# Opening loads issued in one fixed order, by quarters, and the samples' compression moved behind the token-stationary products

## The chip, the cores and the metric

The kernel runs on one core of one Trainium2 chip. The metric is the device time of one execution in microseconds (us). Engines are named as in the profile: PE is TensorE (PEld its weight loads), DVE is VectorE, ACT is ScalarE, POOL is GpSimd, SP is SyncE, which here does little else than issue DMAs. Every engine works through its own list of instructions in order; a list is fixed when the program is built.

## The reference, cut to what matters

One layer of a decoder trunk, for a prompt of 1024 tokens and 8 samples of 4 tokens (1056 tokens, width 1024), all in float32. Of it the change concerns the opening and what reads its results:

```
sh1, sc1, g1, sh2, sc2, g2 = split(silu(c) @ W_ada + b_ada)     # per sequence: the prompt and 8 samples
u = x * (1 + sc1) + sh1
proj = u @ W_in                                                  # q, k, v, gates ... of two head groups
def compress_kv(kv, pe, w1, w2):                                 # blocks of 32 rows, stride 16
    hid = gelu(einsum(blocks(kv) + pe, w1))                      # 2048 -> 256, for k and for v
    return einsum(hid, w2)                                       # 256 -> 64
```

For the samples `compress_kv` runs over the cached rows: `cache_cmp_kv` holds pages of 128 rows, and `page_table` names two pages for each sample, 16 in all. The compressed keys and values are then attended together with selected blocks from another paged cache, a window, and the sample's own rows. Behind that come an mLSTM head group, an output projection, a layer norm and a feed-forward block.

## The kernel before

The opening (lines 213 to 303) is one stretch of code without a planner; a list scheduler orders each engine's instructions from it, by data and by buffers.

The activations `u` are kept transposed, 128 channels on the partitions, in two float32r parts whose sum is u: `uh` (rounded) and `ul` (the rest), each 128 x 8 x 1056. `split` (lines 48 to 51) makes such a pair: ACT casts, DVE subtracts. The same is done to every weight tile (`wt..h`, `wt..l`), and a product is taken as three: uh times high, ul times high, uh times low.

Channels come in four quarters, q = 0 to 3, each of the channel tiles q and q + 4. For a quarter, `ada_steps` (from line 140) loads four tiles `wada` of 512 KB and multiplies them with silu(c) on PE; the result is copied by ACT (`adasb`), transposed by PE (`adat`) and given its bias by DVE (`adaT`, then `sc1p` = 1 + scale). Then three chunks of x (384, 384 and 288 tokens, buffers `xk`) are loaded, scaled and shifted by ACT and DVE, and split into uh and ul. The narrow weight `w_a` (1024 x 288: one K and V branch and all gates) is loaded in four pieces of neighbouring channel tiles in the first quarter, and split into `ah` and `al`, 288 KB a piece.

Two things are computed from this. The token-stationary products `pA` (line 298): nine token tiles, each u (128 tokens as weights) times w_a, 24 matmuls of 288 columns, ordered so that a quarter can be used as soon as it is there; results leave through `vst` to DRAM (`d_v`) and into `gn`. And the samples' compression: `hidS` (line 277), per s (0 for keys, 1 for values) 16 products of w1 with the cached rows for two halves of the hidden layer. Its rows stand in `kv` (128 x 2 x 2 x 8 x 130), filled from the 16 cache pages (`kvr`, two pages in a buffer, four buffers) by copies on DVE and ACT. w1 is loaded in four halves of 1 MB into three buffers. For s = 0 the rows are taken in two pieces of columns (64 and 65), for s = 1 at once (129, times two heads: 258 columns). A float32 matmul shows as two passes in the profile. `gelu2` follows, and `cmp_k`, `cmp_v` (`pkS`, `pvS`) multiply by w2.

Every DMA of the opening is issued by SP, but for eight of the 16 cache pages, which ACT issues. A page's address is first read from the page table into a register. One sequence of DMAs shares eight completion counters in turn, so a DMA waits on SP until the one eight before it has landed. Behind a DMA that waits, all later ones of that engine's list wait too.

Behind the opening come the projections: `proj` takes tile by tile of W_in (order 14 to 19, 12, 13, then 20, 4, 0, 8, ...), 24 matmuls for each of three token chunks, as `pj14_0`, `pj14_1`, `pj14_2` and so on (line 354); `next_weights` loads a tile (512 KB into the single buffer `wst`) one tile ahead, and two pairs of split buffers hold it. Between the projections stand the gates' chain, the next part of ada (`ada10` to `ada13`, line 149, loaded behind the bias row's store `d_rb` and its broadcast `d_rt`), and the samples' attention: scores `SS0`, `SS1` (lines 831 to 844) for two groups of samples, each from four tiles `kb` and a value tile `SV` that take 48 loads in all (lines 839 to 842), then transposes (`ptS`, `ptT`), values (`oS`, `oT`) and an output (`mN`). Projection tiles 12 and 13 give the prompt's compressed rows, `hid` (line 492), for which `d_ck` is stored and read back as `cmpT`.

## Time and profile before

| | us |
|---|---|
| median of 3 runs | 1577.49 |
| lowest and highest run | 1574.25 and 1582.03 |
| the profiled execution | 1580.96 |
| its span in the trace | 1579.2 |

| stretch of the span | what runs on PE |
|---|---|
| 0 to 11.8 us | nothing |
| 11.8 to 51 us | hidS, with ada of the quarters in between |
| 42 to 92 us | pA, quarter by quarter |
| 92 to 183 us | projection tiles 14 to 19, second part of ada in between |
| 183 to 300 us | tiles 12, 13, 20, ..., samples' attention, prompt's compression, third part of ada |

A row of the timeline gives start, length, engine, line, operation, output and inputs, how many instructions are merged in it, and in brackets the idle time of the engine ahead of it with what ended it. A row of the windows gives a stretch, its length, busy time and count of PE, PEld, DVE, ACT and POOL, then the granted TensorE clock (1.00 is full), the busy share of the 16 DMA engines and GB/s. A row of the waits gives who waited for whom, the total, how often, and the longest.

### The profile page before, as it was taken

How to read it: one execution, taken by the hardware profiler on the slowest of the kernel's cores; microseconds unless marked ns; L12 is line 12 of the kernel's file. 1: busy time of each engine (PE TensorE's matmuls, PEld its weight loads, DVE VectorE, ACT ScalarE, POOL GpSimd, SP SyncE). 2: the span in 40 equal slices, each digit the busy share in tenths (PEclk: the TensorE clock that was granted, in tenths of full speed). 3: DMA queues.
4: the chain of work that ended last, by engine and by line, in shares of the span. 5: the costliest groups of instructions: out<-in, count | busy, mean ns of one | idle time of the engine just before them, and what ended most of it. 6: DMA issues, size and time to landing. Idle time of an engine off the chain costs nothing.

```text
span 1579.2 us, 30041 instructions
## 1 busy us (share of the span) xinstructions
PE 1494.8 (95%) x11647; PEld 1436.4 (91%) x11647; DVE 1072.5 (68%) x2366; ACT 629.0 (40%) x1258; POOL 308.6 (20%) x383
## 2 busy tenths in 40 slices
PE   6899999999999999899998799999999999998976
PEld 6789988899999998798897799999999999998975
DVE  2521131386776678977688887676768878889888
ACT  2422132375655566645367322222226433332301
POOL 0000000143224243443103300000001121103244
PEclk9989999999999999999999899999999999999988
DMA  9767566421020323323564566233315241412222
GB/s 300 267 210 241 138 203 218 138 74 47 26 81 17 110 58 113 89 68 105 169 214 155 171 225 208 97 107 109 109 69 191 99 148 57 148 55 82 82 86 84
DMA packets 112985, 204.11 MB, mean 129 GB/s; under 512 B 18529, under 2 KB 63498, under 8 KB 111914
## 3 DMA queue, kind: packets, MB, share of 16 engines
q1 hardware_dynamic: 111546, 200.87, 39.3%
q8 instruction: 92, 1.51, 0.4%
q10 hardware_dynamic: 1296, 1.31, 0.2%
q14 instruction: 51, 0.42, 0.1%
HBM read 162.95 MB, written 46.07 MB: 132 GB/s over the span
## 4 chain that ended last, share of the span: by engine, by line
PE 76%; DVE 13%; DMA 5%; issue 3%; ACT 2%; SPq 1%; POOL 0%; DVEq 0%; ACTq 0%
PE p L1308 19%; PE pj L354 16%; PE pd L1543 11%; PE po L354 6%; PE o L1060 4%; PE pt L1019 4%; PE S L979 4%; DMA wada<-in_w_ada 2%; DVE oplT L51 2%; DVE ophT L51 2%; PE pA L298 2%; PE hidS L277 2%; DVE A L1554 2%; DVE acc L1548 1%; PE ada L149 1%
## 5 line engine op out<-in xcount | busy, mean ns | idle before, releaser
L1543 PE MATMUL pd<-oplT,ophT 128*128 128x264 f32 x2352 | 292.3, 287 | 8.5 <-DVE acc L1548 4.4
L1543 PEld LDWEIGHTS pd<-oplT,ophT 128*128 128x128 f32 x2352 | 291.3, 190 | 9.4 <-DVE ophT L51 4.7
L1002 POOL TENSOR_SCALAR P<-P,l,sg 128x64 f32<-128x64 f32 (+8 forms) x192 | 129.0, 686 | 175.1 <-DVE l L999 156.3
L51 DVE TENSOR_TENSOR PTl<-pt,PTh 128x512 fp32r<-128x512 f32 (+1 forms) x160 | 102.0, 643 | 31.6 <-ACT PTh L50 31.1
L996 ACT ACTIVATE P<-P,mn 128x640 f32<-128x640 f32 (+7 forms) x128 | 94.4, 738 | 68.8 <-DVE mn L823 65.7
L354 PE MATMUL pj<-uh,wt_l 128*128 128x384 f32 (+1 forms) x576 | 120.3, 333 | 0.0
L50 ACT CAST PTh<-pt 128x512 fp32r<-128x512 f32 (+1 forms) x160 | 86.8, 550 | 79.9 <-PE pt L1019 79.0
L1554 POOL TENSOR_TENSOR A<-A,A 128x1024 f32<-128x1024 f32 x7 | 24.1, 3454 | 478.1 <-DVE ophT L51 478.1
L354 PE MATMUL pj<-uh,wt_h 128*128 128x384 f32 (+1 forms) x576 | 115.8, 331 | 1.1 <-ACT rw L468 1.1
L354 PE MATMUL pj<-ul,wt_h 128*128 128x384 f32 (+1 forms) x576 | 116.5, 329 | 0.0
L50 ACT CAST ophT<-A 128x1024 fp32r<-128x1024 f32 x49 | 51.3, 1051 | 139.7 <-PE pd L1543 92.0
L354 PEld LDWEIGHTS pj<-uh,wt_l 128*128 128x128 f32 x576 | 95.7, 190 | 2.9 <-issue 2.4
L354 PEld LDWEIGHTS pj<-uh,wt_h 128*128 128x128 f32 x576 | 93.5, 189 | 3.6 <-issue 1.6
L1019 PE MATMUL pt<-ident,P 128*128 128x128 f32 x592 | 95.5, 275 | 1.1 <-POOL P L1002 1.0
L354 PEld LDWEIGHTS pj<-ul,wt_h 128*128 128x128 f32 x576 | 94.5, 188 | 2.1 <-issue 1.6
L1548 DVE TENSOR_TENSOR acc<-acc,pd 128x264 f32<-128x264 f32 (+1 forms) x126 | 61.7, 513 | 27.6 <-PE pd L1543 27.6
L1060 PE MATMUL o<-PTh,V 128*128 128x256 f32 x264 | 78.9, 306 | 0.5 <-DVE ob L1079 0.4
L1060 PE MATMUL o<-PTl,V 128*128 128x256 f32 x264 | 72.7, 296 | 3.0 <-DVE PTl L51 2.6
L1019 PEld LDWEIGHTS pt<-ident,P 128*128 128x128 f32 x592 | 70.0, 141 | 4.5 <-POOL P L1002 1.8
L51 DVE TENSOR_TENSOR oplT<-B,oplT 128x1056 fp32r<-128x1056 f32 x49 | 72.5, 1479 | 0.4 <-ACT oplT L50 0.2
L979 PE MATMUL S<-K,QH 128*128 128x512 f32 (+3 forms) x200 | 71.6, 362 | 0.9 <-DVE mn L823 0.7
L51 DVE TENSOR_TENSOR ophT<-A,ophT 128x1024 fp32r<-128x1024 f32 x49 | 66.0, 1349 | 8.7 <-ACT ophT L50 8.7
(1095 smaller groups left out, 3465.6 us busy)
## 6 DMA issues: line engine op xcount, KB each, us to landing
wada<-in_w_ada SPq DMA_DIRECT2D x48, 512.0 KB
aw<-in_w_up SPq DMA_DIRECT2D x32, 512.0 KB
d_r<-C SPq DMA_DIRECT2D x62, 264.0 KB
B<-d_r SPq DMA_DIRECT2D x28, 528.0 KB
A<-in_w_down SPq DMA_DIRECT2D x28, 512.0 KB
wst<-in_w_t SPq DMA_DIRECT2D x24, 512.0 KB
wst<-in_w_out SPq DMA_DIRECT2D x24, 512.0 KB
w<-in_cmp_w SPq DMA_DIRECT2D x4, 1024.0 KB
```

Source lines behind the costliest of these rows:

```text
L50: nc.scalar.copy(hi, src)
L51: nc.vector.tensor_tensor(out=lo, in0=src, in1=hi.bitcast(F32), op=ALU.subtract)
L354: PE.matmul(ps[:, 0:n], lhsT=a[:, k, :], rhs=b[:, k, t0:t0 + n], start=(i == 0 and k == 0), stop=(i == 2 and k == 7))
L979: PE.matmul(S[:, 0:w], lhsT=Q[:, r], rhs=K[j][:, k0 + c0:k0 + c0 + w], start=(i == 0), stop=(i == 1))
L996: ACT.activation(P[:, o:o + n], P[:, o:o + n], AF.Exp, bias=mn[:, br:br + 1], scale=-1.0, accum_out=l[:, br:br + 1])
L1002: POOL.tensor_scalar(P[:, a:b], P[:, a:b], l[:, x:x + 1], sg[:, qb, y:y + 1], op0=ALU.mult, op1=ALU.mult)
L1019: PE.transpose(pt[:, 256 * x + 128 * e:256 * x + 128 * e + 128], P[:, o:o + 128], ident)
L1060: PE.matmul(op, lhsT=vv, rhs=ps[e][:, 256 * x:256 * x + 256], start=(x0 + x == 0 and e == 0), stop=(x0 + x == len(bl) - 1 and e == 1))
L1308: PE.matmul(ps[:, 0:HH], lhsT=w[a][:, k], rhs=ops[name][b][:, k, HH * h:HH * h + HH], start=(i == 0 and k == 0), stop=(i == 2 and k == 3))
L1543: PE.matmul(ps[h][:, 0:HH], lhsT=x[:, 128 * m:128 * m + 128], rhs=y[:, HH * h:HH * h + HH], start=(i == 0), stop=(i == len(mms) - 1))
L1548: DVE.tensor_tensor(out=out, in0=out, in1=x, op=ALU.add)
L1554: eng.tensor_tensor(out=r[out], in0=r[a], in1=r[b], op=op)
```

## The change

One chain of issue is added: `ordered` issues a DMA on SP behind the previous DMA of the chain. The opening's large loads all go through it: the four ada tiles, the three x chunks and one piece of w_a for each quarter, then the weights of projection tiles 14 and 15, then the position rows, the 16 cache pages with three of w1's halves between them, and the last half. The pages are all issued by SP. w_a is cut by quarters (channel tiles q and q + 4) in place of neighbouring tiles. The x buffers become six in place of four. The compression `hidS` stands behind the token-stationary products, and for s = 0 takes its 129 columns at once.

```diff
+    chain = []
+    def ordered(*a):
+        with tc.issue_after(chain[-1]) if chain else ExitStack():
+            chain.append(SP.dma_start(*a).ins)
...
-                SP.dma_start(w, io["w_ada"][G, c0, :, k:k + 2])
+                (SP.dma_start if G else ordered)(w, io["w_ada"][G, c0, :, k:k + 2])
...
-    WB, XB = 4, 4
+    WB, XB = 4, 6
...
-        SP.dma_start(w1[s, hf], io["cmp_w1"][:, s, 8 * hf:8 * hf + 8])
-    load_w1(0, 0)
+        ordered(w1[s, hf], io["cmp_w1"][:, s, 8 * hf:8 * hf + 8])
+    def load_caches():
+        pe_ = mk(p0, [128, 2, 2, 8, 2], F32, "pe_")
+        ordered(pe_, io["peT"])
+        DVE.tensor_copy(kvx[:, :, 128:130], pe_.rearrange("p s g c n -> p (s g c) n"))
+        for i in range(16):
+            if i % 5 == 4:
+                load_w1(*((0, 0), (0, 1), (1, 0))[i // 5])
+            page = SP.value_load(pt_sb[0:1, i:i + 1], min_val=0, max_val=19)
+            if i % 2 == 0:
+                kr = mk(p0, [128, 2, 32, 8], F32, "kvr", bufs=4, name=f"kvr{i}")
+            ordered(kr[:, i % 2], io["cache_c"][bass.ds(page, 1)].rearrange("o p (x n) -> p (o x) n", n=8))
+            if i % 2:
+                o = kvx[:, :, 8 * i - 8:8 * i + 8].rearrange("p x (a n) -> p a x n", a=2)
+                (DVE.tensor_copy if i % 4 == 1 else ACT.copy)(o, kr)
+        load_w1(1, 1)
+        SP.dma_start(w2, io["cmp_w2"])
...
-    for i in range(16):
-        e = ACT if i % 2 else SP
-        page = e.value_load(pt_sb[0:1, i:i + 1], min_val=0, max_val=19)
...
-        if i == 6:
-            load_w1(0, 1)
...
+    def next_weights(mt, load=SP.dma_start):
...
-        if q == 0:
-            load_w1(1, 0)
...
-            SP.dma_start(xk[:, :, 0:n], io["xT"][:, q::4, t0:t0 + n])
+            ordered(xk[:, :, 0:n], io["xT"][:, q::4, t0:t0 + n])
...
-        if q == 0:
-            for k in range(0, 8, 2):
-                st = mk(p0, [128, 2, 384], F32, "xk", bufs=XB, name=f"wa{k}")[:, :, 0:288]
-                SP.dma_start(st, io["w_a"][:, k:k + 2])
-                split(nc, ah[:, k:k + 2], al[:, k:k + 2], st)
-        if q == 0:
-            load_w1(1, 1)
-            SP.dma_start(w2, io["cmp_w2"])
-    for s in range(2):
...
-        for n0, n in ((0, 64), (64, 65)) if s == 0 else ((0, 129),):
...
+        st = mk(p0, [128, 2, 384], F32, "xk", bufs=XB, name=f"wa{q}")[:, :, 0:288]
+        ordered(st, io["w_a"][:, q::4])
+        split(nc, ah[:, q::4], al[:, q::4], st)
+    next_weights(14, ordered)
+    load_caches()
...
         SP.dma_start(d_v[t0:t0 + m], vst[0:m])
+    for s in range(2):
...
+        for n0, n in ((0, 129),):
```

The lists of the engines move as follows. A row gives the line, the operation, the output and inputs (the program's names with a buffer number) and the shape. In the changed program the lines stand seven further down, and an ordered DMA bears line 132.

ACT, the fourth quarter of u, before: `adasb03` is the copy of ada's result, `xk30` to `xk32` the three chunks of x, `gu0` belongs to the compression.

```order
L50 CAST uh_119<-xk22_532 128x2x288
L152 COPY adasb03_582<-ada03_540 128x128
L255 ACTIVATE xk30_587<-xk30_587,adaT_93,sc1p_103 128x384
L255 ACTIVATE xk31_593<-xk31_593,adaT_93,sc1p_103 128x384
L255 ACTIVATE xk32_599<-xk32_599,adaT_93,sc1p_103 128x256
L183 ACTIVATE gu0_677<-gu0_677 128x516
L50 CAST uh_119<-xk30_587 128x2x384
```

The same place on ACT now, where `wa3` is the fourth piece of w_a and `wst` the weights of projection tile 14:

```order
L50 CAST uh_119<-xk22_336 128x2x288
L50 CAST ah_132<-wa3_415 128x2x288
L159 COPY adasb03_390<-ada03_348 128x128
L50 CAST wt14_h_421<-wst_419 128x1024
L283 ACTIVATE xk30_395<-xk30_395,adaT_93,sc1p_103 128x384
L283 ACTIVATE xk31_401<-xk31_401,adaT_93,sc1p_103 128x384
L283 ACTIVATE xk32_407<-xk32_407,adaT_93,sc1p_103 128x256
L50 CAST uh_119<-xk30_395 128x2x384
```

The cast of the w_a piece stands ahead of ada's copy and the cast of tile 14's weights ahead of the scaling of x. DVE at the same place now:

```order
L51 TENSOR_TENSOR ul_120<-xk22_336,uh_119 128x2x288
L51 TENSOR_TENSOR al_133<-wa3_415,ah_132 128x2x288
L162 TENSOR_TENSOR adaT_93<-adat03_349,badaT_94 128x4x9
L51 TENSOR_TENSOR wt14_l_422<-wst_419,wt14_h_421 128x1024
L278 TENSOR_SCALAR sc1p_103<-adaT_93 128x2x9
L285 TENSOR_SCALAR xk30_395<-xk30_395,sc1p_103,adaT_93 128x384
```

Both splits stand among the steps that lead to the scaled x, with `sc1p` behind tile 14's; before, no weight split stood between `adaT` and `sc1p` of this quarter.

PE, the end of the token-stationary products, before (`pA8` is the last token tile, `prb` the bias row's product):

```order
L298 MATMUL pA8_961<-ah_315,ul_120 32x288 x2
L310 MATMUL prb_994<-oh_992,rb_115 8x384
L191 MATMUL pkS_1000<-hidS_317,w2_113 64x128 x2
L354 MATMUL pj14_0_1049<-uh_119,wt14_h_1039 128x384 x8
L354 MATMUL pj14_0_1049<-ul_120,wt14_h_1039 128x384 x8
L354 MATMUL pj14_0_1049<-uh_119,wt14_l_1040 128x384 x5
```

PE at the same place now:

```order
L308 MATMUL pA8_853<-ah_132,ul_120 32x288 x2
L361 MATMUL pj14_0_1017<-uh_119,wt14_h_421 128x384 x8
L361 MATMUL pj14_0_1017<-ul_120,wt14_h_421 128x384 x8
L361 MATMUL pj14_0_1017<-uh_119,wt14_l_422 128x384 x7
L319 MATMUL hidS00_882<-kv_130,w100_478 128x258 x3
L319 MATMUL hidS01_883<-kv_130,w100_478 128x258 x3
```

After these two rows come 58 more of hidS, one by one; then the rest of tile 14's first chunk and all of its second, `prb`, `pkS` and `pvS`, and only then its third. The matmuls of ada10, which stood within tile 14's third chunk, stand within tile 15's second.

SP, the samples' attention, before: `wst_2239` is the load of projection tile 13's weights, `kb` and `SV` are the attention's loads.

```order
L840 DMA SV0_1894<-in_cache_s 128x128
L789 DMA qr_1853<-d_q_81 64x4x32
L841 DMA kb02_1988<-in_cache_w 128x256
L842 DMA SV0_1894<-in_cache_w 128x256 x2
L842 DMA SV1_2064<-in_cache_w 128x256 x4
L334 DMA wst_2239<-in_w_t 128x1024
L470 DMA d_ck_83<-rw12_0_2298 128x384
L839 ISA
L839 DMA kb03_1997<-in_cache_s 128x128
```

SP now, around the load of tile 13's weights (`wst_2207`):

```order
L846 DMA kb13_2135<-in_cache_s 128x128
L847 ISA
L847 DMA SV1_2032<-in_cache_s 128x128
L848 DMA kb13_2135<-in_cache_w 128x256
L849 DMA SV1_2032<-in_cache_w 128x256
L253 DMA wst_2207<-in_w_t 128x1024
L477 DMA d_ck_83<-rw12_0_2266 128x384
L477 DMA d_ck_83<-rw12_1_2318 128x384
```

The load stood ahead of `kb03` and all of the second group's `kb`; now it stands behind all 48 loads. On PE the scores, the first group's values and `kb13` stand ahead of tile 13's first matmul in the same way.

More of the change, by code (lines that the diff above doesn't have):

```diff
@@ L215, in _body @@
     w1 = {}
[L216 removed]
+    WB, XB = 4, 6
+    kvx = kv.rearrange("p s g c n -> p (s g c) n")
     def load_w1(s, hf):
         w1[s, hf] = mk(p0, [128, 8, 256], F32, "w1", bufs=3, name=f"w1{s}{hf}")
[L220 to L227 removed]
@@ new lines, in _body, with weights @@
+    SP.dma_start(badaT, io["badaT"])
+    def weights(src, name, stage=None, tag="wst", bufs=1, load=SP.dma_start):
+        st = mk(stage or wp, [128, 1024], F32, tag, bufs=bufs, name="wst")
+        load(st, src)
+        h = mk(wp, [128, 8, 128], F32R, "wh", bufs=2, name=name + "h")
+        l = mk(wp, [128, 8, 128], F32R, "wl", bufs=2, name=name + "l")
+        split(nc, h, l, st.rearrange("p (k c) -> p k c", k=8))
+        return h, l
+    tile_order = [14, 15, 16, 17, 18, 19, 12, 13] + [x + h for h in range(4) for x in (20, 4, 0, 8)]
@@ L241, in _body @@
+    ahead = {}
+    def next_weights(mt, load=SP.dma_start):
+        i = tile_order.index(mt)
+        for x in tile_order[i:i + 2]:
+            if x not in ahead:
+                ahead[x] = weights(io["w_t"][x], f"wt{x}_", load=load)
+        return ahead[mt]
     ah = mk(pA, [128, 8, 288], F32R, "ah")
@@ L303, in _body @@
         SP.dma_start(d_v[t0:t0 + m], vst[0:m])
+    for s in range(2):
+        ph = [mk(ps0, [128, 512], F32, "ha"[s], bufs=2, name=f"hidS{s}{ht}") for ht in range(2)]
+        for n0, n in ((0, 129),):
+            for c in range(16):
+                for ht in range(2):
+                    PE.matmul(ph[ht][:, 0:258].rearrange("p (g n) -> p g n", g=2)[:, :, n0:n0 + n],
+                              lhsT=w1[s, c // 8][:, c % 8, 128 * ht:128 * ht + 128],
+                              rhs=kv[:, s, :, c % 8, n0 + c // 8:n0 + c // 8 + n],
+                              start=(c == 0), stop=(c == 15))
+        for ht in range(2):
+            ACT.copy(pehid[:, s, ht:ht + 1], ph[ht][:, 128:129])
+            ACT.activation(hidS[:, s, ht].rearrange("p g n -> p (g n)"), ph[ht][:, 0:258], AF.Identity,
+                           bias=pehid[:, s, ht:ht + 1])
+        gu = mk(p0, [128, 2, 384], F32, "xk", bufs=XB, name=f"gu{s}")
+        gelu2(gu.rearrange("p a b -> p (a b)")[:, 0:516], hidS[:, s].rearrange("p b c d -> p (b c d)"))
     DVE.memset(rb[32:33], 1.0)
@@ L330, in _body @@
     mlg = mk(ce, [128, 4], F32, "mlg")
-    def weights(src, name, stage=None, tag="wst", bufs=1):
-        st = mk(stage or wp, [128, 1024], F32, tag, bufs=bufs, name="wst")
-        SP.dma_start(st, src)
-        h = mk(wp, [128, 8, 128], F32R, "wh", bufs=2, name=name + "h")
-        l = mk(wp, [128, 8, 128], F32R, "wl", bufs=2, name=name + "l")
-        split(nc, h, l, st.rearrange("p (k c) -> p k c", k=8))
-        return h, l
-    tile_order = [14, 15, 16, 17, 18, 19, 12, 13] + [x + h for h in range(4) for x in (20, 4, 0, 8)]
-    ahead = {}
-    def next_weights(mt):
-        i = tile_order.index(mt)
-        for x in tile_order[i:i + 2]:
-            if x not in ahead:
-                ahead[x] = weights(io["w_t"][x], f"wt{x}_")
-        return ahead[mt]
     def mm24_steps(ps, w, xh, xl, t0, n):
```

23 lines of the change are left out of this document (removed).

## The prediction

> **What bounds the kernel now.** I read the page first, then the table of waits of PE for the first 300 us, then the timelines of PE, ACT, DVE and SP around each place that the change touches.
>
> ```profile
> span 1579.2 us, 30041 instructions
> PE 1494.8 (95%) x11647; PEld 1436.4 (91%) x11647; DVE 1072.5 (68%) x2366; ACT 629.0 (40%) x1258; POOL 308.6 (20%) x383
> ```
>
> PE is busy for 95% of the span. Only stretches in which PE idles can give time back, and work that is moved out of them comes back in full. The longest two entries of PE's waits in the first 300 us (reason, total, times, longest):
>
> ```profile
> PE hidS L277 <- ACT kv L236: 11.8, 1, 11.8
> PE ada L149 <- DMA wada<-in_w_ada: 8.5, 8, 2.6
> ```
>
> With the 3.8 us at 75.80 below, and without the 3.8 us of the w_ada waits that fall past 240 us, the opening holds some 20 us of idle time. The opening on PE (start, length, count, idle time ahead and its reason):
>
> ```profile
> 44.37 4.62 PE L277 MATMUL hidS<-kv,w 128*128 128x258 f32 x20 [0.41 <-DMA w<-in_cmp_w]
> 48.94 2.77 PE L277 MATMUL hidS<-kv,w 128*128 128x258 f32 x12
> 51.36 0.48 PE L298 MATMUL pA<-ah,uh 128*128 128x288 f32 x1
> 75.80 0.85 PE L298 MATMUL pA<-ah,uh 128*128 128x288 f32 x2 [3.78 <-ACT uh L50]
> 92.46 0.81 PE L310 MATMUL prb<-oh,rb 33*8 33x384 f32 x2
> 104.03 1.30 PE L354 MATMUL pj<-uh,wt_h 128*128 128x288 f32 x8
> 108.88 1.08 PE L149 MATMUL ada<-wada,sil 128*32 128x128 f32 x16 [2.61 <-DMA wada<-in_w_ada]
> ```
>
> The samples' compression (hidS) runs while the loads of w_ada and x come in. From 75.80, where the fourth quarter of u is ready, to 104.03, the first matmul of the last third of projection tile 14, PE does 28.23 us of work without a pause.
>
> **The change, term by term.** *Opening.* All of that 28.23 us is still to be done behind the fourth quarter, and now all of hidS too. The rows above put 32 passes into 44.37 to 51.36, less about 0.1 us of a transpose: 0.215 us each. Both halves of hidS are 128 passes (64 of the 192 go, since the first half is no longer cut in two): 27.5 us. So the mark at 104.03 becomes (start of the fourth quarter) + 28.2 + 27.5, and the opening gains only if that quarter starts before 48.3 us. When does it?
>
> ```profile
> 23.00:43.00 20.00, 18.20 (x181) 15.16 (x179) 6.57 (x13) 6.79 (x13) 0.00 (x0) 1.00 0.97 342
> 43.00:63.00 20.00, 19.59 (x179) 16.75 (x179) 9.17 (x18) 9.18 (x17) 0.00 (x0) 1.00 0.98 352
> 57.00:66.00 9.00, 8.67 (x99) 7.68 (x98) 5.66 (x12) 5.54 (x9) 0.00 (x0) 1.00 1.03 393
> 66.00:70.00 4.00, 4.00 (x48) 3.50 (x50) 1.34 (x5) 1.27 (x2) 0.00 (x0) 1.00 0.85 259
> 1.55 5.06 DMA w<-in_cmp_w
> 4.01 4.09 SPq L233 DMA_DIRECT2D kvr<-in_cache_c  x4
> 31.54 0.67 ACT L50 CAST ah<-wa 128x576 fp32r<-128x576 f32 x1
> 39.24 1.04 ACT L50 CAST wt_h<-wst 128x1024 fp32r<-128x1024 f32 x1 [4.79 <-DMA wst<-in_w_t]
> 40.32 1.23 DVE L51 TENSOR_TENSOR wt_l<-wst,wt_h 128x1024 fp32r<-128x1024 f32 x1 [4.52 <-ACT wt_h L50]
> 70.47 0.27 ACT L152 COPY adasb<-ada 128x128 f32<-128x128 f32 x1 [0.79 <-PE ada L149]
> 72.71 1.80 ACT L255 ACTIVATE xk<-xk,adaT,sc1p 128x384 f32<-128x384 f32 x3 [1.98 <-DVE sc1p L248]
> 74.94 2.13 ACT L50 CAST uh<-xk 128x768 fp32r<-128x768 f32 x3
> ```
>
> The last columns of a window are granted clock, DMA share and GB/s: the DMA engines are already full, at about 347 GB/s. A quarter is four w_ada tiles of 512 KB, 384 + 384 + 288 KB of x and 288 KB of w_a: 3392 KB, four make 13.9 MB, and w2 and the constants (0.4 MB) go among them: 14.3 MB, 41.1 us at 347 GB/s. The first 1 MB load took 5.06 us where its bytes take 3.0, so about 2 us pass ahead of the stream, which starts near 2.0: the last piece of w_a lands at 45.1. SP also reads 29 page numbers between these loads. The four cache loads at 4.01 took 1.02 us each with their reads, of which the DMA is 0.34: 0.68 for one read, and six stand right ahead of that last piece (4.1 us). With nothing covering them it lands at 49.2; I take 47.5.
>
> Behind it the order of ACT and DVE counts. The cast of that piece (0.67) stands ahead of the copy of ada, and the split of weight tile 14, whose 512 KB land 1.5 us later, stands on DVE ahead of sc1p. So the cast of wt_h starts 1.5 us behind w_a, wt_l ends at 1.5 + 1.04 + 1.23 = 3.8, the scaling of x starts at 4.0, and with 1.80 and the first uh (0.8) PE starts 6.5 us behind: at 54.0. The mark is then at 109.7 against 104.03: **+5.7**. Bounds: at 393 GB/s (w_ada alone) 46.8, or -1.5; at the late landing plus a slow second quarter 57, or +8.7.
>
> The load of the next w_ada part waits for the bias row's store again:
>
> ```profile
> 96.00 12.84 DMA wada<-in_w_ada
> ```
>
> It landed 16.4 us behind the matmul prb (92.46 to 108.85). In the new order PE has from prb to that part about 2.9 us of small products (estimate), 24 matmuls of tile 14 (1.30 for eight with an overlapped tail, 3.2 together) and 36 of tile 15 (1.66 for eight at 197.95 below, 6.4 together): 12.5. It waits 3.9 instead of 2.6: **+1.3** (0 to +3).
>
> At nothing I cost the two more xk buffers, the cache issues that leave ACT's queue (ACT is idle there) and the caches' copies on DVE and ACT, which lie beside PE's fourth quarter. The last half of w1 waits on SP for hidS's first quarter, near 82 us, with the small tables behind it; hidS needs it near 95, the tables later still. If that cover goes, rival (c) prices it.
>
> *The samples' scores.* Here the change edits no line, but SP's order moves. Before, weight tile 13 was issued between the groups of kb and SV loads; now it stands behind all 48 of them, and these begin behind the evacuation of tile 19's second third.
>
> ```profile
> 179.38 1.22 PE L354 MATMUL pj<-uh,wt_h 128*128 128x288 f32 x8
> 179.63 0.49 ACT L464 ACTIVATE rw<-pj 128x384 f32<-128x384 f32 x1 [3.71 <-PE pj L354]
> 184.90 1.10 SPq L466 DMA_DIRECT2D d_q<-rw  x2
> 187.56 0.66 SPq L789 DMA_DIRECT2D qr<-d_q  x1
> 191.81 0.38 SPq L334 DMA_DIRECT2D wst<-in_w_t  x1
> 193.25 0.34 SPq L839 DMA_DIRECT2D kb<-in_cache_s  x1
> 195.92 0.33 SPq L839 DMA_DIRECT2D kb<-in_cache_s  x1
> 197.95 1.66 PE L354 MATMUL pj<-uh,wt_h 128*128 128x384 f32 x8 [1.15 <-ACT rw L468]
> 200.07 0.62 PE L844 MATMUL SS<-kb,QF 128*32 128x256 f32 x2
> 208.48 0.53 PE L831 MATMUL SS<-kn,QF 128*128 128x32 f32 x4
> 211.80 0.79 PE L354 MATMUL pj<-uh,wt_h 128*128 128x288 f32 x4
> 221.10 0.38 PE L873 MATMUL oS<-vcS,PTs 128*128 128x128 f32 x2
> 223.06 0.60 PE L492 MATMUL hid<-kvP,w1p 128*128 128x128 f32 x3
> ```
>
> Count from Q, the start of tile 19's last third (179.38 before). Five such issues took 193.25 to 195.92, 0.534 each; 48 take 25.6 us. They start about 3 us behind Q (evacuation, two stores at 0.55, two small loads) and two stores and one qr load (1.8) stand among them: weight tile 13 goes out at Q + 30.4. PE used it 6.14 us after its issue (191.81 to 197.95): Q + 36.5. PE's own work up to there was 18.57 less the wait of 1.15, so 17.4, and the new order puts more ahead of tile 13: kb03 and kb13 (1.1 each), the second scores (208.48 to 211.80: 3.3), transposes (0.4), oS (221.10 to 223.06: 2.0), 7.9 in all. PE runs dry for 36.5 - 25.3 = 11.2 us against 1.15: **+10.0**. Were each issue only its 0.35 us, the 48 would take 16.8 and the wait 2.4: +1.3; with loads that wait for earlier ones, +13.
>
> The Trainium skill, "DMA: Bandwidth & Descriptors", section "Issuing engines are not separate DMA queues", says that the time a sequencer takes to start a DMA is usually small relative to the DMA itself. By that the 48 loads (4.2 MB) would cost their 12 us of transfer and the wait would vanish; the rows, 0.534 us for an issue of 64 KB, speak against it, and the rows decide until the run.
>
> *Clock.* A wait of this length is followed by slow matmuls:
>
> ```profile
> 75.00:81.00 6.00, 5.20 (x22) 5.20 (x23) 5.12 (x8) 2.70 (x5) 0.00 (x0) 0.51 0.04 11
> 81.00:92.00 11.00, 11.00 (x86) 10.50 (x86) 1.95 (x9) 2.60 (x8) 0.26 (x2) 1.00 0.29 95
> 109.00:115.00 6.00, 6.00 (x60) 4.09 (x60) 1.18 (x2) 1.45 (x2) 0.00 (x0) 0.50 1.06 444
> ```
>
> After the 3.8 us wait the granted clock was 0.51 until 81; 22 matmuls took 5.2 us that take 2.8 at 11.00/86: 2.4 us lost. The opening had two such starts and keeps two; tile 13 adds one: **+2.4** (0 to +3). The Trainium skill, "TensorE: Matmul & The Clock Gate", section "Part 1: The HAM clock gate (the "warmup" mystery)", gives about 3.4 us of idleness for the drop and as much work for the return; here 2.61 us were enough and the return took six, so the row differs, and by the page the term would be 1.7.
>
> *Later.* Of the 3.8 us past 240 us: the third part's loads are issued in the same place behind the first samples' output, so I give back 1 us: **-1.0** (-3.8 to +3). From 300 us on PE's order shifts but PE stays full.
>
> **Sum**: +5.7 + 1.3 + 10.0 + 2.4 - 1.0 = +18.4 us. The profiled execution took 1580.96 us (span 1579.2), 3.5 over the median of 1577.49; on its own time that is 1599.4, on the median 1595.9. I predict **1596 us**.
>
> **The rivals.** *(a) The issues are not the limit* (+1.3 at tile 13, no cold start): 5.7 + 1.3 + 1.3 - 1.0 = +7.3, 1584.8. For it: each issue is busy for 0.35 us alone. Against: the gaps between them had no wait. Chance 0.13. *(b) The opening pays*, the other side: the ordered stream runs at the 393 GB/s row, so the quarter starts at 46.8 (-1.5), the wait at 108.88 and its slow clock go (-5.0), tile 13 costs +1.3 and the later waits go (-3.8): -9.0, 1568.5. It decides once the quarter starts before 48.3 and the 48 issues are cheap. Against it: x runs at 259. Chance 0.06. *(c) The caches come too late.* Tile 15's weights wait for tile 14's split (about 51.3), and 6.3 MB of weights and caches follow. At 347 GB/s they land at 71.5, before PE reaches hidS (54.0 + 16.7 + 4.0 = 74.7); at 259 they land at 77.7, PE waits 4 us with the copies and starts cold: +6, 1602. Chance 0.12. *(d) Issue order isn't landing order*, so the quarters overlap and the early ones give PE nothing: the last landing still decides, about +2, 1598. Chance 0.07. The forecast has 0.62.
>
> **How the numbers follow.** About 0.5% (7.9 us) is what a measurement of this kernel can tell from no change. Slower by more holds the forecast, (c) and (d): 0.81; within it (a): 0.13; faster (b): 0.06. The range reaches down past (a), leaves out (b), and reaches up to where most of the upper ends (+8.7, +13, +3) meet: 1582 to 1607.
>
> **What would show it.** Right: PE's fourth quarter near 54 us, hidS as one unbroken stretch of 27 us behind tile 14's first third, its last third near 110, and a PE wait of about 11 us ahead of tile 13 with the granted clock at a half behind it. Wrong: a fourth quarter before 48, weight tile 13 landing before PE has finished the scores, or a wait of hidS for kv.

## The result and the profile after

The changed kernel takes 1601.51 us (median of 4 runs, 1597.61 to 1603.44), the kernel before 1575.87 (4 runs, 1573.01 to 1582.03). The ratio is **1.0144, 95% interval 1.0119 to 1.0168**: slower. (The two medians alone differ by 25.6 us, or 1.0163, inside that interval.) The profiled execution took 1599.99 us, 19.0 more than that of before (1580.96, which lies 5.1 above its median, where this one lies 1.5 below its own), and it is these 19.0 us that can be placed. The page's first lines:

```profile
span 1598.2 us, 29895 instructions
PE 1498.1 (94%) x11583; PEld 1435.8 (90%) x11583; DVE 1081.8 (68%) x2366; ACT 628.5 (39%) x1258; POOL 310.3 (19%) x383
```

PE has 64 instructions fewer (the half of the compression that is no longer cut in two), is busy 3.3 us more, and the span is 19.0 us longer: most of the loss is waiting, and a part is matmuls that run longer. PE's waits in the first 300 us (total, times, longest):

```profile
PE ada L156 <- DMA wada<-in_w_ada: 19.0, 12, 6.2
PE pj L361 <- ACT wt_h L50: 4.9, 1, 4.9
PE SS L838 <- DVE mnS L830: 2.3, 1, 2.3
PE pA L308 <- DVE gn L312: 2.1, 1, 2.1
```

The 11.8 us that PE waited for the compression's caches have gone. In their place it waits longer for w_ada, and the other three entries are new: tile 13's split, and two waits for DVE (mnS, a step of the samples' scores, and gn). PE's timeline of the opening (start, length, count, idle time ahead and its reason):

```profile
54.37 0.85 PE L308 MATMUL pA<-ah,uh 128*128 128x288 f32 x2 [4.27 <-ACT uh L50]
...
64.10 0.53 PE L308 MATMUL pA<-ah,uh 128*128 128x288 f32 x2 [2.14 <-DVE gn L312]
...
77.65 28.00 PE L319 MATMUL hidS<-kv,w 128*128 128x258 f32 x128
...
109.96 0.81 PE L336 MATMUL prb<-oh,rb 33*8 33x384 f32 x2
...
114.01 1.32 PE L361 MATMUL pj<-uh,wt_h 128*128 128x288 f32 x8 [0.53 <-ACT rw L475]
...
125.93 0.64 PE L156 MATMUL ada<-wada,sil 128*32 128x128 f32 x16 [1.47 <-DMA wada<-in_w_ada]
```

The fourth quarter starts at 54.37 instead of 75.80, the compression is one unbroken stretch behind tile 14's first chunk, and tile 14's last third, the mark of the forecast, starts at 114.01 instead of 104.03. What released the fourth quarter stands on ACT and DVE:

```profile
48.11 0.67 ACT L50 CAST ah<-wa 128x576 fp32r<-128x576 f32 x1 [6.50 <-DMA wa<-in_w_a]
48.69 0.26 ACT L159 COPY adasb<-ada 128x128 f32<-128x128 f32 x1
49.37 1.05 ACT L50 CAST wt_h<-wst 128x1024 fp32r<-128x1024 f32 x1 [0.42 <-DMA wst<-in_w_t]
50.45 1.23 DVE L51 TENSOR_TENSOR wt_l<-wst,wt_h 128x1024 fp32r<-128x1024 f32 x1
51.59 0.17 DVE L278 TENSOR_SCALAR sc1p<-adaT 128x18 f32<-128x18 f32 x1
53.50 2.12 ACT L50 CAST uh<-xk 128x768 fp32r<-128x768 f32 x3
63.52 0.43 DVE L245 COPY kv<-kvr 128x512 f32<-128x512 f32 x1 [4.50 <-DMA kvr<-in_cache_c]
63.86 0.18 DVE L312 COPY gn<-pA 128x32 f32<-128x32 f32 x1
```

Up to 53.50 this is the forecast's chain: the last piece of w_a, ada's copy, the split of tile 14, sc1p, u. The last two rows are the cause of the wait at 64.10: DVE stands in order, a cache copy waits 4.50 us for its page, and behind it stands the copy of gn that frees the PSUM buffer PE needs.

The samples' scores on SP, PE and, by window, PE's granted clock (the third column from the right):

```profile
218.16 0.37 SPq L253 DMA_DIRECT2D wst<-in_w_t  x1
209.56 0.60 PE L838 MATMUL SS<-kn,QF 128*128 128x32 f32 x4 [2.29 <-DVE mnS L830]
210.44 1.92 PE L851 MATMUL SS<-kb,QF 128*32 128x256 f32 x4
225.18 2.93 PE L361 MATMUL pj<-uh,wt_h 128*128 128x384 f32 x8 [4.94 <-ACT wt_h L50]
209.00:215.00 6.00, 5.44 (x22) 2.70 (x23) 1.56 (x9) 1.39 (x5) 0.00 (x0) 0.72 0.56 158
225.00:231.00 6.00, 5.82 (x19) 5.83 (x20) 3.59 (x12) 1.77 (x8) 0.00 (x0) 0.52 0.67 184
```

Weight tile 13 goes out behind the 48th cache load; PE waits 4.94 us for its split, and after each of the two waits it runs slowly, from 210.3 to 213.7 us and up to 230.8 (eight matmuls of 384 columns take 2.93 us at 225.18, where before eight took 1.66 at 197.95). SP itself waits for nothing there but 0.4 us for one store: from 196.13 to 218.05 it issues 42 loads one behind the other, 0.52 us each, so neither buffers nor landings hold it.

To place the 19.0 us I use two marks in each trace: **M**, the start of tile 14's last third, and the start of the first product with T4h, a tile of the feed-forward block (899.8 before, 919.3 after). Behind the second, all kernels of this study take 678 to 682 us.

```text
                         before   after   difference
start to M               104.03  114.01   +10.0
M to tile 19's last third 75.35   72.59    -2.8
from there to T4h         720.4   732.7   +12.3
T4h to the end            679.4   678.9    -0.5
```

### The profile page after: what moved, and what is told of

Its sections match the earlier page's. It is cut to its first block, busy times and chain, and to the rows that moved or that the text cites. A ratio compares the mean times of both kernels' runs of the same rounds, so it can differ in the third digit from the quotient of the medians.

```text
span 1598.2 us, 29895 instructions
## 1 busy us (share of the span) xinstructions
PE 1498.1 (94%) x11583; PEld 1435.8 (90%) x11583; DVE 1081.8 (68%) x2366; ACT 628.5 (39%) x1258; POOL 310.3 (19%) x383
## 3 DMA queue, kind: packets, MB, share of 16 engines
q1 hardware_dynamic: 112698, 201.92, 38.6%
## 4 chain that ended last, share of the span: by engine, by line
PE 72%; DVE 15%; DMA 6%; issue 3%; SPq 2%; ACT 2%; POOL 1%; DVEq 0%; ACTq 0%
PE p L1315 19%; PE pj L361 15%; PE pd L1550 11%; PE po L361 6%; PE o L1067 4%; PE pt L1026 3%; PE S L986 3%; DVE oplT L51 2%; PE hidS L319 2%; DVE ophT L51 2%; DVE A L1561 2%; DVE acc L1555 1%; DMA wada<-in_w_ada 1%; PE pd L1644 1%; PE ada L156 1%
## 5 line engine op out<-in xcount | busy, mean ns | idle before, releaser
L1009 POOL TENSOR_SCALAR P<-P,l,sg 128x64 f32<-128x64 f32 (+8 forms) x192 | 132.2, 701 | 174.2 <-DVE l L1006 161.7
L51 DVE TENSOR_TENSOR PTl<-pt,PTh 128x512 fp32r<-128x512 f32 (+1 forms) x160 | 102.4, 642 | 38.6 <-ACT PTh L50 38.2
L361 PE MATMUL pj<-uh,wt_l 128*128 128x384 f32 (+1 forms) x576 | 115.9, 329 | 0.0
```

The costliest lines, as they stand in the source:

```text
L51: nc.vector.tensor_tensor(out=lo, in0=src, in1=hi.bitcast(F32), op=ALU.subtract)
L361: PE.matmul(ps[:, 0:n], lhsT=a[:, k, :], rhs=b[:, k, t0:t0 + n], start=(i == 0 and k == 0), stop=(i == 2 and k == 7))
L1009: POOL.tensor_scalar(P[:, a:b], P[:, a:b], l[:, x:x + 1], sg[:, qb, y:y + 1], op0=ALU.mult, op1=ALU.mult)
```

## The experiments

c1 to c12 have 6 or 12 runs each. Ratios are to the runs of the kernel before in the same session. The last three columns are from one profiled execution each. Runs of one kernel spread (29 of the kernel before: 1570.4 to 1584.9 us), so a difference of a few us in the last column is not shown by it alone.

```text
kernel                          median   ratio [95%]               span     M      M to T4h
before                          1575.87                            1579.2  104.03  795.8
changed                         1601.51  1.0144 [1.0119, 1.0168]   1598.2  114.01  805.3
c1 compression behind only      1611.98  1.0215 [1.0186, 1.0244]   1609.6  126.65  802.1
c2 order of loads only          1610.30  1.0201 [1.0174, 1.0228]   1605.7  136.72  787.9
c3 tile 13 first                1592.79  1.0082 [1.0055, 1.0109]   1594.8  115.97  797.0
c4 w_a first                    1602.31  1.0140 [1.0112, 1.0167]   1600.8  114.02  806.2
c5 tiles 14 and 15 last         1596.46  1.0126 [1.0103, 1.0149]   1593.6  110.42  805.1
c6 caches second                1580.33  1.0029 [1.0012, 1.0046]   1573.3  108.78  784.9
c7 two queues                   1589.49  1.0091 [1.0065, 1.0118]   1588.6  114.19  793.5
c8 before, tile 13 first        1574.93  0.9991 [0.9974, 1.0008]   1571.5  105.15  787.9
c9 pieces                       1574.20  0.9999 [0.9978, 1.0020]   1571.6  101.73  791.3
c10 pieces, weights earlier     1577.99  1.0004 [0.9987, 1.0021]   1576.5  107.84  788.8
c11 repaired                    1582.32  1.0050 [1.0033, 1.0067]   1578.4  108.07  789.8
c12 pieces, tile 13 first       1571.55  0.9969 [0.9958, 0.9981]   1569.7  101.67  789.1
```

### One part alone

c1 is the kernel before with the compression behind the products and nothing else:

```diff
-    for s in range(2):
-        ph = [mk(ps0, [128, 512], F32, "ha"[s], bufs=2, name=f"hidS{s}{ht}") for ht in range(2)]
...
         SP.dma_start(d_v[t0:t0 + m], vst[0:m])
+    for s in range(2):
+        ph = [mk(ps0, [128, 512], F32, "ha"[s], bufs=2, name=f"hidS{s}{ht}") for ht in range(2)]
...
```

> The kernel before with one part of the change alone: the samples' compression (128 passes, 27.5 us) stands behind the token-stationary products; the loads go out as before. Theory A (the load order decides when quarters start, and the compression was what PE did meanwhile): the fourth quarter still starts at about 76 us, because its loads are not earlier, PE has 27.5 us less to do ahead of it, and tile 14's last third starts at 104 + 20 to 27.5 = 124 to 131 us; total about 1600 (1594 to 1606). Rival B (the position costs little, because PE's work is the same and only its order changes): tile 14's last third at 104 to 108, total 1575 to 1581.

Measured: M at 126.65 as theory A has it (+22.6), though the fourth quarter came at 70.23 and not at 76; the total is 6 us above its range. The rest is in the scores, which theory A had left out. PE's waits from 205 to 300 us in c1:

```profile
PE pj L353 <- ACT wt_h L50: 4.5, 1, 4.5
PE SS L830 <- DVE mnS L822: 2.3, 1, 2.3
```

They are the changed kernel's two. So the dry stretch at the scores comes with the *compression's place*, through the order in which the scheduler lists SP's issues, and not with the loads' order. c2 is the other part alone, the changed loads with the compression written ahead of the products (still with all 129 columns at once):

```diff
     next_weights(14, ordered)
     load_caches()
+    for s in range(2):
+        ph = [mk(ps0, [128, 512], F32, "ha"[s], bufs=2, name=f"hidS{s}{ht}") for ht in range(2)]
...
         SP.dma_start(d_v[t0:t0 + m], vst[0:m])
-    for s in range(2):
-        ph = [mk(ps0, [128, 512], F32, "ha"[s], bufs=2, name=f"hidS{s}{ht}") for ht in range(2)]
...
```

> The changed kernel with the other part alone: loads in the fixed order, caches last, and the compression written ahead of the products as before. Theory A: the caches land when they land (the last kv copy at about 74 us), so the place in the text gives nothing back: fourth quarter at 54 to 55, tile 14's last third at 110 to 115, total within 5 us of the changed kernel wherever the scores come out alike. Rival B (the new position of the compression is what costs the opening's 10 us): tile 14's last third back at 104 to 106. The load of weight tile 13 stands in the middle of the cache loads here; if the wait behind all 48 loads is what costs the scores 8 us, a part of that (3 to 6 us) is gone too: 1596 (1590 to 1603).

Measured: neither theory, M at 136.72. PE's timeline of c2:

```profile
49.86 0.85 PE L323 MATMUL pA<-ah,uh 128*128 128x288 f32 x2 [5.16 <-ACT uh L50]
...
73.45 29.62 PE L302 MATMUL hidS<-kv,w 128*128 128x258 f32 x128 [19.67 <-ACT kv L245]
```

The fourth quarter was ready at 49.86, with over 20 us of its products to do, but they stand behind the compression in PE's list, and PE waits 19.67 us for the caches with that work in hand. Each part alone moves M by +22.6 or +32.7, both together by +10.0: with the caches last, the compression has to stand behind the products, and with the compression there, early quarters are what limits the damage.

### The samples' scores

c3 is the changed kernel with one line ahead of the samples' loop, which asks for tile 13's weights there:

```diff
+    next_weights(12)
+
     for h in range(2):
         S = mk(pss_, [128, 1024], F32, "S", bufs=1, name=f"SS{h}")
```

> The changed kernel with weight tile 13 asked for ahead of the samples' 48 cache loads on SP instead of behind them; the opening is untouched. Theory A (SP's issue of 48 loads, 28 us, starves PE): no wait of over 1 us for tile 13's weights, the 4.94 us wait and the second stretch of half-clock matmuls gone, end of the stage 8 us earlier (5 to 12), total 1593 (1589 to 1598). Rival C (the fill work is used up earlier and PE then dries out elsewhere in the stage): waits of the same sum at other places, total 1599 to 1604. Late in the program (from the first transposes of the normalisation to the first product with T4h: 111.7 us in the kernel before, 119.6 in the changed one) theory L, that the 7.9 us come from another order of the engines' instructions there, expects a span that differs from kernel to kernel; its rival, that the earlier delay brings them, expects 119 to 120 for each kernel with the changed opening.

Measured: theory A. SP issues the load ahead of the first cache load, and PE's waits from 198 to 300 us shrink from 8.0 to 2.0 (the 1.5 below and 0.5 for a cache load):

```profile
193.09 0.37 SPq L253 DMA_DIRECT2D wst<-in_w_t  x1
194.91 0.41 SPq L848 DMA_DIRECT2D kb<-in_cache_s  x1
PE pj L361 <- ACT rw L475: 1.5, 1, 1.5
```

M to T4h falls by 8.3 us, to 797.0, which is within 1.2 of the kernel before. c7 leaves tile 13's place and takes the 24 loads into SV off SP's queue:

```diff
-                SP.dma_start(SV[:, 0, b, j], src[:, :, 128:256].rearrange("o p d -> p (o d)"))
+                ACT.dma_start(SV[:, 0, b, j], io["cache_s"][bass.ds(pagea[2 * b + j], 1)][:, :, 128:256].rearrange("o p d -> p (o d)"))
...
-            SP.dma_start(SV[:, 1, b], io["cache_w"][B, :, 256:512].rearrange("p (j d) -> p j d", j=2))
+            ACT.dma_start(SV[:, 1, b], io["cache_w"][B, :, 256:512].rearrange("p (j d) -> p j d", j=2))
```

> The changed kernel with half of the samples' 48 cache loads (those into SV) issued by ACT instead of SP. Theory A (the time to issue, about 0.53 us a load on one queue, is the limit): the loads are all issued within 14 to 18 us instead of 28, and tile 13's weights with them; no wait of over 1.5 us for tile 13; the scores 5 to 9 us earlier, total 1594 (1590 to 1600), less what ACT's 24 issues (12 us) delay. Rival F (the DMA engines' rate is the limit): the loads' landings take the same 28 us, tile 13's wait stays at 4 us or more, total 1599 to 1604.

Measured: theory A, at 1589.49 just below its range. Tile 13 is issued between two groups of cache loads, and PE reaches it without a wait; the longest wait left there is 2.69 us for a cache page:

```profile
206.02 0.37 SPq L253 DMA_DIRECT2D wst<-in_w_t  x1
210.96 0.59 PE L851 MATMUL SS<-kb,QF 128*32 128x256 f32 x2 [2.69 <-DMA kb<-in_cache_s]
211.48 1.67 PE L361 MATMUL pj<-uh,wt_h 128*128 128x384 f32 x8
```

Together with SP's own rows in the changed kernel this says that the issue on one queue, at some 0.53 us a load, starved PE; the DMA engines were not full (a share of 0.56 from 209 to 215 us). One caution: moving the loads also made the scheduler place tile 13's load between them, so c7 alone can't divide the gain between the shorter queue and the better place. c3, where the 48 loads stay on SP, shows that the place alone is enough.

### The chain ahead of the fourth quarter

c4 puts each quarter's piece of w_a ahead of that quarter's other loads:

```diff
+        st = mk(p0, [128, 2, 384], F32, "xk", bufs=XB, name=f"wa{q}")[:, :, 0:288]
+        ordered(st, io["w_a"][:, q::4])
+        split(nc, ah[:, q::4], al[:, q::4], st)
         ada_part(0, q, p0, WB, p0, pa, pt)
...
-        st = mk(p0, [128, 2, 384], F32, "xk", bufs=XB, name=f"wa{q}")[:, :, 0:288]
-        ordered(st, io["w_a"][:, q::4])
-        split(nc, ah[:, q::4], al[:, q::4], st)
```

> The changed kernel with each quarter's piece of w_a loaded ahead of that quarter's other loads instead of behind them; same bytes. Theory A (the stream plus 6.5 us of a chain behind its last piece set the fourth quarter): u's last piece now lands last at about 47.5 us, only its scaling (3 to 4 us) is behind it, the fourth quarter starts at 51 (50 to 52) instead of 54.4, tile 14's last third 3 us earlier at 111, total 1598 (1594 to 1602). Rival D (casts of w_a are not in the way; scaling waits for the modulation's sums anyway): fourth quarter at 54 to 55, no change.

Measured: no change in time, as rival D has it, and the fourth quarter 1.7 us later. Its last steps, by engine, and the wait for gn behind them:

```profile
48.80 1.08 PE L156 MATMUL ada<-wada,sil 128*32 128x128 f32 x32
49.95 0.27 ACT L159 COPY adasb<-ada 128x128 f32<-128x128 f32 x1 [7.21 <-PE ada L156]
53.31 0.17 DVE L281 TENSOR_SCALAR sc1p<-adaT 128x18 f32<-128x18 f32 x1
56.09 0.85 PE L308 MATMUL pA<-ah,uh 128*128 128x288 f32 x2 [4.05 <-ACT uh L50]
64.11 0.53 PE L308 MATMUL pA<-ah,uh 128*128 128x288 f32 x2 [0.60 <-DVE gn L312]
```

The bytes of w_a were not what held the quarter. Its w_ada sums stand behind the third quarter's products on PE, so adasb is made only at 49.95, and from there to sc1p another 3.4 us pass, in which ada's transpose waits for its turn on PE and DVE splits tile 14. That M stays all the same (114.02) shows what comes next in line: the cache page that holds gn is copied at 63.53, as in the changed kernel (63.52), so PE starts later and waits less, 0.60 us instead of 2.14. c5 takes that split out of the way:

```diff
-    next_weights(14, ordered)
     load_caches()
+    next_weights(14, ordered)
```

> The changed kernel with the load of weight tiles 14 and 15, and so their splits on ACT and DVE, behind the caches instead of ahead of them. Theory A' (formed on the run with w_a first, where the fourth quarter came no earlier because the modulation's last sums and the splits of tile 14 stand ahead of sc1p): without wt14_h (1.05 us on ACT) and wt14_l (1.23 us on DVE) ahead of it, sc1p is made 1.5 to 2.5 us after adasb, the fourth quarter starts at 52.3 (51.5 to 53) instead of 54.4, tile 14's last third 2 us earlier, total 1599 (1596 to 1603). Rival D (the stream alone sets it): fourth quarter at 54 to 55, no change.

Measured: theory A' in direction; the quarter gains less than expected (1.4 us against 2.1), M more (3.6 against 2).

```profile
49.53 0.18 DVE L278 TENSOR_SCALAR sc1p<-adaT 128x18 f32<-128x18 f32 x1
52.97 0.82 PE L308 MATMUL pA<-ah,uh 128*128 128x288 f32 x2 [3.85 <-ACT uh L50]
60.62 0.54 PE L308 MATMUL pA<-ah,uh 128*128 128x288 f32 x2 [1.10 <-DVE gn L312]
```

adasb to sc1p takes 1.6 us instead of 2.9, the quarter starts 1.4 us earlier, the wait for gn is 1.04 shorter since the caches are no longer behind a megabyte of weights, and M is 3.6 us earlier. The remaining 1.1 us go with slow matmuls that end sooner: the granted clock is back at 56.4 us, in the changed kernel at 60.1.

### A suspicion about the late part

In the changed kernel the stretch from the first transposes of the normalisation to T4h takes 119.5 us, in the kernel before 111.8, though the change is 700 us away. c2 and c7 have PE's rows there in the order of the kernel before (113.2 and 114.2 us), as c9 and c10 do (112.1 and 111.9); c1 and c3 to c6 don't (118.6 to 119.9). Late openings don't decide it, as c2 and c7 have them too. c8 gives the kernel before another order there by moving one load (c3's two lines):

> The kernel before, whole, with one load moved: weight tile 13 is asked for ahead of the samples' cache loads. Nothing of the change is in it. Theory L (the late stretch, from the first normalisation transposes to the first product with T4h, takes 112 to 114 us in one order of PE's and ACT's instructions and 118.5 to 120 in another, and which order the scheduler lists hangs on small shifts far ahead): here the late rows stand in the order of the run with the caches behind the first quarter (118.6 us), so the stretch takes 118 to 120 although the opening and its end are those of the kernel before; the scores gain 0 to 2 us; total 1582 (1578 to 1585), slower than before. Its rival (the delay of the changed opening brings the 7 us): the stretch takes 112 as before, total 1575 to 1577.

The first transposes and the first product with T4h, before and then in c8 (the two times in a row are the first and the last start):

```profile
L1245 PE MATMUL pn<-ident,y x72: 270/272/284, 788.1 to 843.3; 128*128 128x128 f32 x64, 128*32 128x128 f32 x8
L1308 PE MATMUL p<-T4h,ah x128: 281/285/291, 899.8 to 1192.3; 128*128 128x264 f32 x128
```

```profile
L1247 PE MATMUL pn<-ident,y x72: 270/272/285, 775.1 to 836.2; 128*128 128x128 f32 x64, 128*32 128x128 f32 x8
L1310 PE MATMUL p<-T4h,ah x128: 279/285/288, 893.1 to 1185.5; 128*128 128x264 f32 x128
```

Half of the theory held and its price fell: the stretch takes 118.0 us, as the order foretold, but it begins 13.0 us earlier, and c8 is not slower (0.9991). Some 6 of the 13.0 us may lie between the two executions alone: their spans differ by 7.7 us, the medians by 1.8. The longer late stretch goes together with a shorter one ahead of it, so it must not be counted as a loss by itself, and only M to T4h as a whole compares.

### All of it, and a version that beats both

c11 has c3's and c5's edits in the changed kernel, and the cache copies on POOL:

```diff
-                (DVE.tensor_copy if i % 4 == 1 else ACT.copy)(o, kr)
+                POOL.tensor_copy(o, kr)
```

> The changed kernel with three repairs: weight tiles 14 and 15 loaded behind the caches, tile 13 asked for ahead of the samples' loads, and the cache copies on POOL, so that no copy waits for a cache page on DVE ahead of the products' gates. The loads' order (caches last) and the compression's place are the change's. Theory A (the change loses the opening's part by the late fourth quarter and the scores' part by tile 13's load, and nothing else): fourth quarter at 53, no wait for gn, tile 14's last third at 107 to 110 against 104 before; from there to the end the kernel before's time within 3 us; total 1583 (1578 to 1588), 3 to 8 us over the kernel before. A rival (a third loss that is still unnamed, in the stretch from 300 us on): from tile 14's last third to the end over 5 us more than before, total 1590 or more.

Measured: 1582.32, as expected. PE's timeline of c11:

```profile
51.79 0.54 PE L308 MATMUL pA<-ah,uh 128*128 128x288 f32 x2 [3.44 <-ACT uh L50]
...
108.07 1.33 PE L361 MATMUL pj<-uh,wt_h 128*128 128x288 f32 x8 [0.53 <-ACT rw L475]
```

No wait for gn is left. From the fourth quarter to M are 56.3 us, of which 0.53 is waiting. M stays 4.0 us behind the kernel before and from there to the end c11 takes 4.9 us less, yet the runs still give 1.0050: the profiled execution was the fastest of c11's six, and that of before lay 5.1 above its median. With these three repairs the caches' place last in the stream costs little, but it brings no gain.

c6 takes the other way: the caches behind the *first* quarter, the compression ahead of the products, tile 13 first.

```diff
         split(nc, ah[:, q::4], al[:, q::4], st)
+        if q == 0:
+            load_caches()
     next_weights(14, ordered)
-    load_caches()
```

> The fixed order of loads with the caches and the compression's weights behind the first quarter (instead of behind the fourth), the compression written ahead of the products as in the kernel before, and weight tile 13 asked for ahead of the samples' loads. Theory A (loads must bring PE's filling early): PE starts at 6 instead of 11.8 us, waits some 5 us more for the caches behind the first quarter, then has no wait of over 3 us before tile 14; its last third at 98 to 104; scores without a wait for tile 13; and because the order of the rest follows the kernel before's, the late stretch (first normalisation transposes to the first product with T4h) takes 112 us. Total 1574 (1568 to 1581). Rival E (any fixed order on one queue costs, since 20 MB stand in one stream and PE's order is fixed at build): waits for the later quarters of over 8 us, last third at 108 or later, total 1582 or more.

Measured: 1580.33, at the edge of theory A's range, with rival E's late M (108.78). On PE, on SP, and in two windows:

```profile
31.62 4.67 PE L303 MATMUL hidS<-kv,w 128*128 128x258 f32 x10 [12.14 <-ACT kv L245]
41.76 0.33 SPq L132 DMA_DIRECT2D w<-in_cmp_w  x1
31.00:37.00 6.00, 5.38 (x13) 4.24 (x14) 0.17 (x1) 0.57 (x1) 0.00 (x0) 1.00 0.14 34
35.00:40.00 5.00, 5.00 (x19) 4.11 (x18) 0.00 (x0) 0.00 (x0) 0.00 (x0) 1.00 0.00 0
```

PE waits 12.14 us for all 16 pages, since the compression now begins with all columns at once; and the fourth piece of its weights has to wait for one of three buffers until 41.76, with the whole ordered stream behind it, so that from 35 to 40 us nothing moves at all. c9 goes against both: the first half in two pieces of columns again, the fourth piece behind the second quarter (it still goes out at 41.62, but the second quarter's loads now stand ahead of it), and c7's second queue in place of tile 13 first.

```diff
-        load_w1(1, 1)
-        SP.dma_start(w2, io["cmp_w2"])
...
+        if q == 1:
+            load_w1(1, 1)
+            SP.dma_start(w2, io["cmp_w2"])
...
-        for n0, n in ((0, 129),):
+        for n0, n in ((0, 64), (64, 65)) if s == 0 else ((0, 129),):
```

> A version meant to beat both: fixed order with the caches behind the first quarter, the compression ahead of the products and its first half in two pieces of 64 and 65 columns as in the kernel before (so that it can start when half of the caches are in), the fourth piece of its weights behind the second quarter (it held the order up until a buffer came free), and SV's loads on ACT's queue. Theory A: PE's wait for the caches 4 to 9 us instead of 12.1, tile 14's last third at 99 to 104, no dry stretch in the scores, the late stretch 112 to 114 (its rows stand in the kernel before's order): total 1568 (1562 to 1574). Rival E (what is won in the opening is lost to waits for the later quarters): last third at 105 or later, total 1576 to 1582.

> As the run with the pieces, with the second part of the compression's first weights behind the sixth cache page instead of the ninth, so that the first 64 columns have both weight parts by then. Theory A: PE's wait for the caches 2 to 3 us shorter than in that run (w's second part lands before the eighth page), last third 1 to 3 us earlier, total 1566 (1561 to 1573). Rival: the wait is for the eighth page, not for the weights, which come later here by one load's time; no difference (within 2 us).

c9: M at 101.73 and PE's waits for the caches of 4.8 us as expected, but a total of 1574.20, just above its range, that can't be told from the kernel before. c10, with a load's place changed (`if i in (4, 6, 14):` instead of every fifth), missed. The first 64 columns wait for the eighth page, as its rival has it, and that page now comes later: PE starts them at 23.62 us, in c9 at 21.22. The buffer that the fourth piece needs comes free later too, so the ordered stream stands still again, until 45.61 us, and this window of c10 shows a DMA share of 0.02:

```profile
41.00:46.00 5.00, 5.00 (x40) 4.79 (x39) 2.75 (x9) 2.75 (x5) 0.00 (x0) 1.00 0.02 2
```

The third quarter's w_ada comes late by it, and M is 6.1 us later. c12 is c9 with all loads on SP and tile 13 first:

> The run with the pieces, with the samples' loads all on SP again and weight tile 13 asked for ahead of them. Opening as there (tile 14's last third at 101 to 103); from there to the first product with T4h the time of the two other runs with tile 13 first and the kernel before's place of the compression (784.9 and 788 us, against 791.3 with the pieces and 795.8 before). Theory A (the terms add): 101.7 + 786 + 679 = 1567 us of span, total 1569 (1564 to 1574), faster than the kernel before by 0.4%. Rival (what a stage wins is lost where its filling work would have gone): total 1574 to 1579.

```profile
20.42 9.24 PE L304 MATMUL hidS<-kv,w 128*128 128x128 f32 x64 [1.04 <-ACT kv L245]
```

Measured: 1571.55, ratio 0.9969 (0.9958 to 0.9981), faster than the kernel before by a small but measurable step, and than the changed one. The terms add nearly as expected: M 2.4 us earlier, M to T4h 6.7 us shorter. The medians differ by less, 4.6 us, again because the profiled execution of the kernel before was a slow one.

## Why the prediction was right, point by point

The forecast was 18.4 us slower, at 1596; measured were 19.0 us between the profiled executions, 25.6 between the medians, and a median of 1601.5. The direction and the two main mechanisms hold. That 18.4 and 19.0 are so near is in part luck: terms miss on opposite sides, and the profiled execution of the kernel before was a slow one.

**Opening: +5.7 forecast, +10.0 measured.** The start of the fourth quarter was right (54.0 against 54.37), and so were the arrival of w_a's last piece (47.5, picked between 45.1 and 49.2, against 48.1) and the 6.5 us behind it (6.3). "All of that 28.23 us is still to be done, and now all of hidS too" held as well: 55.7 us forecast, 56.3 in c11. What failed is the sentence that cost the caches' copies at nothing because they "lie beside PE's fourth quarter". In the changed kernel the same stretch takes 59.6: the copy that waits for its page holds gn, and PE with it, for 2.14 us; c11 and c5 show it, where this wait is gone or halved. Another 0.53 us go to ACT's copy `rw` at 113.48, which stands behind a copy for the compression (c11 has it too). The last 1.2 us are spread: half of them lie in the small products from prb on (3.5 us to the wait at 114.01, 3.0 before), the rest in the other products, at most 0.5 us in each kind. The measured +10.0 lies above the bound of +8.7, which had no term for a copy standing in the way.

**ada10: +1.3 forecast, -2.8 measured.** The load lands 16.0 us behind prb (16.4 before), but PE had more to do up to there than the 12.5 us counted: 16.0 less the waits of 0.53 and 1.47 are 14.0. The wait fell to 1.5 us, and PE's slow matmuls after it disappeared.

**The samples' scores: +10.0 and +2.4 for the clock forecast.** The mechanism was right, and c3 and c7 show it by two different cures. Counted from tile 19's last third, tile 13's load went out 31.6 us behind it (30.4 forecast) and was used at 38.6 (36.5). PE waited 4.94 us ahead of tile 13, not 11.2, and 3.1 us more in shorter waits on the way, for which the prediction had no term (2.29 of them for DVE's mnS). Less these 8.0, it had 30.6 us to do up to there where the prediction counted 25.3; part of that are slow matmuls behind the 2.29 us wait, the rest stays open. Two slow stretches stand there instead of one. With the one that left at ada10 the net is one more, as the clock term had it, but by luck: neither the second nor the one that left was foreseen. Without the starved tile (c3) the stretch from tile 19's last third to T4h is 9.4 us shorter (723.3 against 732.7); the two terms together had 12.4. Rival (a), that the issues are not the limit, is refuted by c3 and by SP's rows. By the Trainium skill, "DMA: Bandwidth & Descriptors", section "Issuing engines are not separate DMA queues", the time to start a DMA is usually small beside the transfer; for these loads of 64 and 128 KB it was not, at 0.53 us each. What the prediction didn't see is why SP's order moved: c1 shows that the compression's place does it alone.

**Later: -1.0 forecast.** From tile 19's last third on, the rest of the difference is 12.3 - 9.4 = 2.9, and -0.5 behind T4h. The third w_ada part's waits (3.8 us) did go; something else gave them back. M to T4h spreads from 785 to 797 us over the kernels that don't wait for tile 13's weights, with the same work in another order; which part of the order costs what was not settled, and a part of the spread is that of single executions.

Rivals (b) and (c) did not come: the compression never waits for kv (its last copy starts at 74.25 and takes 0.64, PE begins at 77.65), and the quarter was not early enough. For (d), the quarters came in order, at 16.6 to 54.4 us.

## What to carry to other kernels

Work that fills a wait is worth its full length, so before moving it, find what the engine does instead at that place; here the two halves of the change cost 23 and 33 us of opening alone, and 10 together. In a queue that serves in order, one item that can't go yet (a copy whose page is late, a load whose buffer is taken, 48 loads ahead of one weight tile) holds all behind it: look at what stands behind the waiting item, not only at the item. Where a scheduler lists the instructions, an edit changes the order hundreds of microseconds away, so compare whole stretches between fixed marks before calling a late difference a loss.

## What was unexpected of the hardware

Whether slow matmuls follow a wait can't be told from its length alone. After 2.29 us at the scores (changed kernel, 209.56) four matmuls of kb took 1.92 us where four such take 1.05 at 199.56; after 2.14 us (64.10) nothing slowed. In c11, behind the 3.44 us wait shown above, PE ran at full speed for about 1 us and only then slowly until 56.2 (two like matmuls take 0.43 us at 52.16 and 0.68 at 53.52). Three windows of c11 (PE's clock is the third column from the right):

```profile
49.43:52.83 3.40, 1.04 (x8) 1.04 (x9) 2.76 (x7) 3.40 (x6) 0.62 (x1) 1.00 0.92 355
52.85:56.24 3.39, 3.39 (x17) 3.39 (x16) 1.42 (x2) 0.20 (x1) 1.10 (x2) 0.50 0.94 322
56.26:59.60 3.34, 3.34 (x27) 3.34 (x26) 0.96 (x5) 1.48 (x5) 0.13 (x1) 1.00 0.98 302
```

The times at which the granted clock changes say why. In each of the 14 traces all its changes (290 in all) lie whole multiples of 3.413 us apart, to within 0.01 us: in the changed kernel at 39.6, 46.5, 53.3, 60.1, 210.3, 213.7, 224.0 and 230.8 us, in c11 at 39.2, 42.6, 52.8 and 56.3. So the clock changes only at the end of such a stretch, and what counts is how much of the stretch a wait fills. The 2.29 us lie whole in the stretch from 206.9 to 210.3, in which PE is busy for 1.12 us, and the clock falls at 210.3. The 2.14 us are cut in two at 63.5; the stretch up to there has 1.85 us of work, and the clock stays. In c11 1.04 us of work stand in the stretch up to 52.8, and the clock falls there, 1 us after PE has gone on. How little work it takes is not settled: in the kernel before the clock falls at 316.4 behind a stretch with 2.33 us of it.

And the clock column can mislead: it shows 1.00 up to the first change that the trace has on record. In c6 matmuls of the compression start 0.43 us apart behind the 12.14 us wait and 0.22 from 37.7 on, while the window from 31 to 37 us shows 1.00; the first change on record there is the rise at 37.5. The wait alone did not make them slow, as PE was slow ahead of it too (at 18 us products pA start 0.24 us apart, 0.13 when warm). The length of like matmuls is the surer sign.
